# A hybrid GLA/S5/mLSTM layer: head pieces resumed by stated waiting times instead of fixed program points

## The chip, the cores and the metric

The kernel runs on one core of one Trainium2 chip. The metric is the device time of one execution in microseconds (us). A profiled execution is also there; its span is the time from its first to its last instruction.

## The reference, cut to what matters

One layer on 1024 tokens of width 1024, all in fp32. The mixer projects the normed input to many parts, runs three branches over them, and adds the branches up with sigmoid gates; a convolutional FFN follows.

```python
z = u @ w_in
(g_q, g_k, g_v, g_lr, g_r, s_u, m_q, m_k, m_v, m_i, m_f, m_o, gate_pre) = jnp.split(z, ...)
o = gla_chunked(heads(g_q), heads(g_k), heads(g_v), heads(log_a))      # 4 heads, chunks of 64
o = rms_norm(o, gla_norm) * silu(heads(g_r))
y = gelu(s5_scan(s_u, ...))                 # 32 groups: complex diagonal recurrence, 64 states each
y = y * sigmoid(y @ s5_w_glu + s5_b_glu)
qk = silu(causal_dwconv(concatenate([m_q, m_k]), ml_conv_w, ml_conv_b))
hid = mlstm_chunked(q_ml, k_ml, heads(m_v), m_i + ml_b_i, m_f + ml_b_f)    # 4 heads
hid = sigmoid(heads(m_o)) * hid
merged = gates[0] * (o @ gla_w_proj) + gates[1] * (y @ s5_w_proj) + gates[2] * (hid @ ml_w_proj)
x = x + rms_norm(merged @ w_out);  x = x + rms_norm(conv_ffn(rms_norm(x)))
```

## The kernel before, in words

Every projection is done in three fp32r matmuls, from a rounded part ("hi") and a rest ("lo") of each operand. ACT casts hi and DVE subtracts to get lo; `split` (lines 87 to 89) does both, and `load_w` (line 91) loads a weight tile by DMA and splits it whole. The raw tile has one buffer, hi and lo have two each.

The stretch that the change touches goes from about 76 to 616 us. TensorE has there a *main stream* of projections, in this order: the S5 input (`su_half` twice, token-major, line 864); for each of four GLA heads K, Q and the output gate R (`chan_major`, line 117: 8 blocks of 6 matmuls of 512 columns, 48 in all, into one PSUM pair of two banks); the mLSTM values (two halves of 8 token tiles, `tok_mm`, line 179); for each of four mLSTM heads K, Q and the output gate O; then the merge gates, in pairs of 128 columns, first by plain products (96 matmuls a pair), later in a seven-product form (84 matmuls a pair, `run`). PSUM has eight banks: two pairs (`big`), three single banks (`bank`) and one for S5 (`bank2`).

Beside it run *pieces*: Python generators that are stepped at fixed places of the main stream and trace a few instructions each time, until their next `yield`.
- `gla_gates(h)` (line 329), not a generator: two matmuls into a PSUM pair, then DVE and ACT work on 1024 columns that gives the decay factors E. It is traced whole, at one place.
- `gla_inner` (line 359): transposes of k (line 368), scores (374), chunk states (384, with fifteen DVE state updates in line 394), inner outputs (400), outer outputs (410), a sum on DVE (412), a square on POOL (413), the norm (415 to 417), and last the output transposes (423). It is stepped four times with TensorE work.
- `ml_gates` (line 444): a chain of tiny matmuls and DVE instructions (498 and 495 among them) that gives the mLSTM weights.
- `conv_silu2` (line 522): the convolution, one ACT instruction, three on DVE that read the PSUM pair (line 527), a tanh and a last one on DVE; traced whole behind each K and Q of the mLSTM.
- `ml_inner` (line 543): transposes (552), scores (559), states (568, 571), outputs (579, 580, with 582 and 584 on DVE) and output transposes (597). Stepped four times.
- `s5_set(s)` (line 702), eight sets of four groups: seven small loads; products on POOL (723 to 737); two small scalings on DVE (732, 733); transposes (742, 746); the kernel block (752, 753); the rotation angles, with rounding on DVE (767, 768) and the sums on POOL (`sub` and `add`, lines 610 and 607), two sines on ACT (773, 774), a square on POOL and a scaling on DVE (776); the input product (781); the *rotation* on DVE: nine products and sums (line 789) and eight scans (799); the products 812 and 816; and after each second set two output transposes (825) with a gelu.

What sets the order: `advance()` steps every running generator once, after each projection and after each fourth token tile; `extra()` steps S5 alone, at every projection's middle, as often as a rate of 0.6 allows:

```python
def extra():
    credit[0] += RATE
    if credit[0] >= 1.0 and s5 in running:
        credit[0] -= 1.0
        step([s5])
```

The compiler's scheduling pass then places each engine's instructions: by program order, but an instruction whose inputs are late by the pass's own times can be overtaken by later ones. The gates' loop goes on by plain products while any generator runs (`while running`, line 1051).

Of the kernel before, what the change touches and what calls it, by code (L numbers as in the profile page):

```python
# [18 lines left out]
S = 1024  # L19
# [3 lines left out]
H = 4  # L23
# [9 lines left out]
def hybrid_layer(ctx: ExitStack, tc: tile.TileContext, a, out, dbg=None):  # L33
# [53 lines left out]
    def split(hi, lo, src):  # L87
        return (ordered("act", act.copy(hi, src)),  # L88
                ordered("dve", dve.tensor_tensor(lo, src, hi.bitcast(F32), op=ALU.subtract)))  # L89

    def load_w(srcs, rows, cols, late=None, keep=None):
# [5 lines left out]
        if late is None:  # L97
            split(hi, lo, raw)
        else:
            late.append((hi, lo, raw))  # L100
# [16 lines left out]
    def chan_major(wt, i, xh, xl, ps=None, ns=(0, 1)):  # L117
# [14 lines left out]
    midway = []  # L132
# [7 lines left out]
    RATE = 0.6  # L140
# [38 lines left out]
    def tok_mm(wt, i, lhs, put, c0, to=None):  # L179
        hi, lo = wt  # L180
        ps = big()[:, 0, 0:hi.shape[2]] if to is None else to([128, hi.shape[2]])
        for k in range(8):
            for p, (l, r) in enumerate(((0, hi), (1, hi), (0, lo))):
                pe.matmul(ps, lhs(l, k, i), r[:, k, :],
                          start=(k == 0 and p == 0), stop=(k == 7 and p == 2))
        put(i, c0, ps)

# [141 lines left out]
    def gla_gates(h):  # L329
        ps = big()  # L330
        for n in range(2):
            pe.matmul(ps[:, n, :], wg[:, h * 128:(h + 1) * 128], lrx[:, n * 512:(n + 1) * 512],
                      start=True, stop=True)
        z = flat(ps)
        bias = cols[:, 40 + h:41 + h]
        ax, mn, b = g([128, S]), g([128, S]), g([128, S])
        dve.tensor_scalar(mn, z, bias, 0.0, op0=ALU.add, op1=ALU.min)
        dve.scalar_tensor_tensor(out=ax, in0=mn, scalar=2.0, in1=z, op0=ALU.mult, op1=ALU.subtract)
# [12 lines left out]
        return ax, b, mn, dec  # L351

    def silu2(ps):
# [3 lines left out]
        return t  # L357

    def gla_inner(h, E, r2):
        qd, ki, kd, dec = E  # L360
        vt = g([128, 8, 128])
        sync.dma_start(vt, v_dram[0][:, :, h * 128:(h + 1) * 128].rearrange("i p e -> p i e"))
        kt = g([128, 8, 128])
        for hf in range(2):
# [4 lines left out]
            act.copy(kt[:, hf * 4:hf * 4 + 4, :], ps)  # L369
        for hf in range(2):  # L370
# [5 lines left out]
        yield  # L376
        st = [g([128, 8, 128]) for _ in range(2)]
        pool.memset(st[0][:, 0, :], 0.0)
        for o in range(2):
            for p in range(2):  # L380
# [7 lines left out]
                else:  # L388
                    act.copy(st[o][:, 2::2, :], kv[:, 0:3, :])
                    if o == 0:  # L390
                        act.copy(st[1][:, 0, :], kv[:, 3, :])
            for c in range(o * 8, min(o * 8 + 8, 15)):
# [9 lines left out]
        yield  # L402
        yield
        for hf in range(2):
# [8 lines left out]
            pool.tensor_tensor(sq, oo, oo, op=ALU.mult)  # L413
            ssq = small.tile([128, 4], F32, tag="ssq4", name="ssq4")
            dve.tensor_reduce(ssq, sq, axis=AX.X, op=ALU.add)
            rs = rstd_of(ssq, 4, DH)
            dve.tensor_tensor(oo, oo, rs.unsqueeze(2).to_broadcast([128, 4, 128]), op=ALU.mult)
        yield
        yield
# [24 lines left out]
    def ml_gates():  # L444
# [18 lines left out]
        act.activation(e1, e1, AF.Ln, bias=1.0)  # L463
        dve.tensor_scalar(lf, xf, 0.0, None, op0=ALU.min)
        dve.tensor_tensor(lf, lf, e1, op=ALU.subtract)
        yield
# [9 lines left out]
        yield  # L476
# [6 lines left out]
        yield  # L483
# [12 lines left out]
        yield  # L496
# [10 lines left out]
        yield  # L507
# [14 lines left out]
    def conv_silu2(ps, j):  # L522
        z = flat(ps)
        acc, t = g([128, S]), g([128, S])
        act.activation(acc, z, AF.Identity, scale=cols[:, 24 + j:25 + j], bias=cols[:, 32 + j:33 + j])
        for k in range(1, 4):
# [3 lines left out]
        act.activation(t, acc, AF.Tanh, scale=0.5)  # L530
        dve.scalar_tensor_tensor(out=t, in0=t, scalar=1.0, in1=acc, op0=ALU.add, op1=ALU.mult)
        return t
# [10 lines left out]
    def ml_inner(h, wm, qm, km, tm):  # L543
# [4 lines left out]
        for e in range(2):  # L548
            ps = bank([128, 4, 128])
            for q in range(4):  # L550
# [3 lines left out]
                              kwx[:, h, e * 4:e * 4 + 4].unsqueeze(2).to_broadcast([128, 4, 128]), op=ALU.mult)  # L554
        for e in range(2):
# [6 lines left out]
        yield  # L562
        st = g([128, 8, 129])
        pool.memset(st[:, 0, :], 0.0)
        for j0, n in ((0, 3), (3, 3), (6, 1)):
# [3 lines left out]
            act.copy(st[:, j0 + 1:j0 + 1 + n, :], kv[:, 0:n, :])  # L569
            for j in range(j0, j0 + n):  # L570
                dve.scalar_tensor_tensor(out=st[:, j + 1, :], in0=st[:, j, :], scalar=scx[:, h, j:j + 1],
                                         in1=st[:, j + 1, :], op0=ALU.mult, op1=ALU.add)
        yield
        nn = g([128, 8, 129])
        for j0, n in ((0, 3), (3, 3), (6, 2)):
# [8 lines left out]
            dve.tensor_tensor(dst, dst, pa[:, 0:n, :], op=ALU.add)  # L584
        rd = small.tile([128, 8], F32, tag="rd", name="rd")
# [7 lines left out]
        yield  # L593
        for e in range(2):
# [4 lines left out]
            dve.scalar_tensor_tensor(out=tm[0][:, t], in0=tm[0][:, t], scalar=1.0,  # L599
                                     in1=po.rearrange("p a b -> p (a b)"), op0=ALU.add, op1=ALU.mult)  # L600
        sync.dma_start(o_dram[2][h], tm[0])
# [99 lines left out]

    def s5_set(s):
# [11 lines left out]
        bst = s5p.tile([128, 2, 4, 16], F32, tag="bst", name="bst", bufs=1)  # L714
        for i, nm, p0 in ((0, "s5_b_re", 0), (0, "s5_b_im", 64), (1, "s5_b_im", 0), (1, "s5_b_re", 64)):
            sync.dma_start(bst[p0:p0 + 64, i], a[nm][0, gs].rearrange("g p h -> p g h"))
        cl = s5p.tile([64, 3, 64], F32, tag="cl", name="cl", bufs=1)
        for i, nm in ((0, "s5_c_re"), (1, "s5_c_im"), (2, "s5_c_re")):
            sync.dma_start(cl[:, i, :], a[nm][0, gs].rearrange("g h p -> (g h) p"))
# [7 lines left out]
        pool.tensor_copy(zr_, zt.rearrange("p j (g h) -> p g j h", h=16)[:, :, ::-1, :])  # L727
        ps = bank2([128, 2, 64])
# [3 lines left out]
        dve.tensor_scalar(c01[:, 0].rearrange("p g h -> p (g h)"), ps[:, 0, :], sgn[:, 0:1], None, op0=ALU.mult)  # L732
# [844 lines left out]
```

## Time and profile before

| | us |
|---|---|
| median of 3 runs (lowest, highest) | 1746.9 (1745.06, 1747.82) |
| the profiled execution's own time | 1745.36 |
| its span | 1743.6 |
| TensorE, DVE, ACT, POOL busy | 1689.5, 1151.8, 646.8, 398.1 |
| mean granted TensorE clock | 0.994 of 2.4 GHz |

Engines are named PE (TensorE), PEld (TensorE's weight load), DVE (VectorE), ACT (ScalarE), POOL (GpSimd) and SPq (SyncE's DMA queue). A line such as L816 is a line of the kernel. A fp32 tile is named by its pool's tag: z is a PSUM pair, m a single bank, q a buffer of S5 (in PSUM or SBUF), g one of the 14 head buffers. A row of the waits reads: this engine and line waited for that engine and line; total, times, longest. A row of busy times gives, behind the stretch and its length, busy us (and instructions) of PE, PEld, DVE, ACT and POOL, then the mean granted clock, the DMA share and GB/s. In a row of groups, "busy, mean ns of one" is followed by the idle time just before and what ended it.

### The profile page before, as it was taken

How to read it: one execution, taken by the hardware profiler on the slowest of the kernel's cores; microseconds unless marked ns; L12 is line 12 of the kernel's file. 1: busy time of each engine (PE TensorE's matmuls, PEld its weight loads, DVE VectorE, ACT ScalarE, POOL GpSimd, SP SyncE). 2: the span in 40 equal slices, each digit the busy share in tenths (PEclk: the TensorE clock that was granted, in tenths of full speed). 3: DMA queues.
4: the chain of work that ended last, by engine and by line, in shares of the span. 5: the costliest groups of instructions: out<-in, count | busy, mean ns of one | idle time of the engine just before them, and what ended most of it. 6: DMA issues, size and time to landing. Idle time of an engine off the chain costs nothing. (4 is left out here: it accounts for less than half of the span.)

```text
span 1743.6 us, 21877 instructions
## 1 busy us (share of the span) xinstructions
PE 1689.5 (97%) x8556; PEld 1412.1 (81%) x8556; DVE 1151.8 (66%) x1462; ACT 646.8 (37%) x940; POOL 398.1 (23%) x437
## 2 busy tenths in 40 slices
PE   6999998999999999999899999999999999999997
PEld 6997877897888888888688788788888888888886
DVE  4426677536667675444745654967777787669987
ACT  4544533333443223333510233433333333344343
POOL 1163243333334012222000011022322332101021
PEclk9999999999999999999899999999999999999999
DMA  6242131333141322434674643222232223483161
GB/s 205 68 113 60 43 88 34 92 91 89 23 133 49 97 85 85 127 115 145 222 249 144 217 142 125 73 73 82 76 90 79 85 73 97 169 283 127 55 218 54
DMA packets 196440, 195.10 MB, mean 112 GB/s; under 512 B 29208, under 2 KB 154305, under 8 KB 196337
## 3 DMA queue, kind: packets, MB, share of 16 engines
q1 hardware_dynamic: 195456, 190.56, 34.9%
q0 software_dynamic: 880, 3.15, 0.5%
q8 instruction: 67, 1.10, 0.3%
q14 instruction: 37, 0.30, 0.1%
HBM read 143.32 MB, written 48.25 MB: 110 GB/s over the span
## 5 line engine op out<-in xcount | busy, mean ns | idle before, releaser
L89 DVE TENSOR_TENSOR lo<-raw,hi 128x512 fp32r<-128x512 f32 (+3 forms) x163 | 174.7, 1091 | 132.0 <-ACT hi L88 129.3
L88 ACT CAST hi<-raw 128x512 fp32r<-128x512 f32 (+3 forms) x163 | 130.2, 833 | 283.1 <-PE z L126 122.0
L983 POOL TENSOR_TENSOR raw<-raw 128x512 f32<-128x512 f32 x28 | 39.5, 1412 | 472.4 <-DVE lo L89 472.4
L126 PE MATMUL z<-ohl,hi 128*128 128x512 f32 x448 | 123.3, 398 | 6.1 <-ACT ohl L1098 6.1
L126 PEld LDWEIGHTS z<-ohl,hi 128*128 128x128 f32 x448 | 85.5, 191 | 26.1 <-ACT ohl L1098 6.5
L68 POOL TENSOR_SCALAR rstd<-ssq 128x1 f32<-128x1 f32 (+1 forms) x32 | 9.3, 292 | 316.4 <-ACT x L1262 262.5
L126 PE MATMUL z<-u0h,hi 128*128 128x512 f32 x240 | 79.5, 408 | 1.4 <-DVE g L894 1.4
L126 PE MATMUL z<-u0h,lo 128*128 128x512 f32 x240 | 77.0, 398 | 0.0
L126 PE MATMUL z<-u0l,hi 128*128 128x512 f32 x240 | 76.5, 398 | 0.0
L126 PE MATMUL z<-u1h,hi 128*128 128x512 f32 x240 | 75.4, 395 | 0.0
L126 PE MATMUL z<-u1h,lo 128*128 128x512 f32 x240 | 75.0, 392 | 0.0
L126 PE MATMUL z<-u1l,hi 128*128 128x512 f32 x240 | 74.9, 393 | 0.0
L126 PE MATMUL z<-ohl,lo 128*128 128x512 f32 x224 | 70.2, 396 | 0.0
L1303 DVE SCALAR_TENSOR_TENSOR cv<-u,fcol,cv 128x1023 f32<-128x1023 f32 (+1 forms) x38 | 48.7, 1280 | 23.9 <-ACT cv L1301 23.9
L89 DVE TENSOR_TENSOR xl<-raw,xh 128x512 fp32r<-128x512 f32 x57 | 51.8, 935 | 11.2 <-ACT xh L88 8.3
L1301 ACT ACTIVATE cv<-u,fcol 128x1024 f32<-128x1024 f32 x19 | 23.6, 1244 | 89.9 <-DVE u L1001 89.9
L789 DVE TENSOR_TENSOR q<-q,q 128x512 f32<-128x512 f32 x72 | 49.5, 714 | 8.7 <-PE q L812 8.3
L126 PEld LDWEIGHTS z<-u0h,lo 128*128 128x128 f32 x240 | 45.3, 190 | 9.7 <-issue 0.2
L126 PEld LDWEIGHTS z<-u1h,lo 128*128 128x128 f32 x240 | 45.1, 188 | 9.8
L126 PEld LDWEIGHTS z<-u1l,hi 128*128 128x128 f32 x240 | 44.9, 188 | 9.9 <-issue 0.2
L126 PEld LDWEIGHTS z<-u0l,hi 128*128 128x128 f32 x240 | 44.8, 189 | 9.6 <-issue 0.4
L126 PEld LDWEIGHTS z<-u1h,hi 128*128 128x128 f32 x240 | 44.5, 188 | 9.3
(561 smaller groups left out, 5006.0 us busy)
## 6 DMA issues: line engine op xcount, KB each, us to landing
raw<-in_w_in_dram SPq DMA_DIRECT2D x48, 512.0 KB, 5.3
pt<-gate SPq DMA_DIRECT2D x24, 512.0 KB, 3.3
raw<-in_ffn_w_up_dram SPq DMA_DIRECT2D x22, 512.0 KB, 4.0
raw<-in_ffn_w_gate_dram SPq DMA_DIRECT2D x22, 512.0 KB, 5.3
h<-cv SPq DMA_DIRECT2D x21, 512.0 KB, 2.6
bx<-in_ffn_w_down_dram SPq DMA_DIRECT2D x15, 512.0 KB, 4.4
by<-in_ffn_w_down_dram SPq DMA_DIRECT2D x15, 512.0 KB, 5.1
gate<-u SPq DMA_DIRECT2D x11, 512.0 KB, 3.0
```

What stands on the lines that cost most here:

```text
L68: pool.tensor_scalar(r, ssq, 1.0 / width, EPS, op0=ALU.mult, op1=ALU.add)
L88: return (ordered("act", act.copy(hi, src)), ordered("dve", dve.tensor_tensor(lo, src, hi.bitcast(F32), op=ALU.subtract)))
L89: ordered("dve", dve.tensor_tensor(lo, src, hi.bitcast(F32), op=ALU.subtract)))
L126: pe.matmul(ps[:, n, :], l[:, k, c], r(k, n), start=(k == 0 and p == 0), stop=(k == nk - 1 and p == 2))
L789: dve.tensor_tensor(o, x, y, op=op)
L983: pool.tensor_tensor(a22, a21, a22, op=ALU.add)
L1301: first = act.activation(cv, src, AF.Identity, scale=fcol[:, 44 + f:45 + f], bias=fcol[:, 66 + f:67 + f])
L1303: ins = dve.scalar_tensor_tensor(out=cv[:, k:], in0=src[:, 0:S - k], scalar=fcol[:, (2 - k) * 22 + f:(2 - k) * 22 + f + 1], in1=cv[:, k:], ...
```

## The change

Each `yield` of a piece now returns the waiting time in us before its next part. A modelled clock `now` is moved on by the main stream (`tick`: 1.37 us per block of six matmuls, 1.45 us per half token tile) and by 0.13 us for each TensorE instruction of a piece. At each tick up to two pieces that are due are resumed. The first TensorE and the first DVE instruction that a resumed piece traces are ordered behind the newest instruction of that engine; the weight splits are left out of this. So pieces can't be placed ahead of where they were traced.

```diff
+            for k in range(0, rows, rows // 2):            # load_w: split by halves
+                ks = slice(k, k + rows // 2)
+                split(hi[:, ks, :], lo[:, ks, :], raw[:, ks, :])
...
-            if k == 3 and midway:                          # chan_major, after each block k
-                midway[0]()
+            tick(6 * len(ns) * 0.114)
...
+    def note(first=None):
+        traced = nc.cur_bb.bb.instructions
+        bound, work = set(), 0.0
+        for ins in traced[seen[0]:]:
+            e = ins.engine
+            if e == mybir.EngineType.PE:
+                work += 0.13
+            if e not in (mybir.EngineType.PE, mybir.EngineType.DVE):
+                continue
+            if first is not None and e not in bound and e in newest:
+                bound.add(e)
+                tc.add_manual_dep(ins, newest[e], ..., reason="turn")
+            if ins.name not in free_:
+                newest[e] = ins.name
+        seen[0] = len(traced)
+        return work
+
+    def resume(turn_):
+        note()
+        try:
+            wait = next(turn_[1])
+        except StopIteration:
+            turns.remove(turn_)
+            wait = 0.0
+        now[0] += note(turn_)
+        turn_[0] = now[0] + wait
+
+    def tick(us):
+        now[0] += us
+        due = sorted((t for t in turns if t[0] <= now[0]), key=lambda t: t[0])
+        for t in due[:2]:
+            resume(t)
```

`gla_gates` becomes a generator. Its projection goes through two single banks of 512 columns instead of a pair; after the first exp and ln it waits 8.0. `gla_inner` is cut into more parts: k transposes, 4.0, scores, 1.5, states of the first half, 2.5, their updates and the second half's states, 2.5, updates and inner outputs, 10.0, outer outputs, 3.5, sums of squares, 7.0, norm, 5.0, output transposes. The square is made by ACT instead of POOL. `ml_gates` waits 6.0 once and 5.0 between its steps. `silu2` waits 2.5 between its tanh and its DVE instruction.

```diff
+    def conv_silu2(ps, j, to):
...
         act.activation(acc, z, AF.Identity, scale=cols[:, 24 + j:25 + j], bias=cols[:, 32 + j:33 + j])
+        yield 2.5
         for k in range(1, 4):
             dve.scalar_tensor_tensor(out=acc[:, k:], in0=z[:, 0:S - k], ...
         act.activation(t, acc, AF.Tanh, scale=0.5)
+        yield 8.0
         dve.scalar_tensor_tensor(out=t, in0=t, scalar=1.0, in1=acc, op0=ALU.add, op1=ALU.mult)
+        yield 3.0
+        to.append(t)
```

`ml_inner` begins with the convolution of K; then come the transposes, 1.5, the scores (when q is there), 1.5, states, 3.0, state updates, 5.0, the outputs of three, three and two chunks with 1.5 between, 7.0, and the output transposes, when the output gate is there. In `s5_set` the angles move to the front, the rotation's preparation goes to DVE and ACT, and the parts get times:

```diff
+        mul(ph, iob.to_broadcast(sq_), t_hi[:, gs].unsqueeze(2).to_broadcast(sq_))
+        mul(pl, iob.to_broadcast(sq_), t_lo[:, gs].unsqueeze(2).to_broadcast(sq_))
...
+        yield 4.0
+        for i in range(2):
+            dve.tensor_scalar(pk, ph, magic, None, op0=ALU.add)
+            dve.tensor_scalar(pk, pk, -magic, None, op0=ALU.add)
+            dve.tensor_tensor(ph, ph, pk, op=ALU.subtract)
+            if i == 0:
+                dve.tensor_tensor(ph, ph, pl, op=ALU.add)
...
+        act.activation(cs, cs, AF.Square)
+        act.activation(cs, cs, AF.Identity, scale=-2.0, bias=1.0)
...
-        dve.tensor_scalar(c01[:, 0].rearrange("p g h -> p (g h)"), ps[:, 0, :], sgn[:, 0:1], None, op0=ALU.mult)
+        act.mul(c01[:, 0].rearrange("p g h -> p (g h)"), ps[:, 0, :], sgn[:, 0:1])
...
+        yield 8.0
...
-            sub(ph, ph, pk)
-            if i == 0:
-                add(ph, ph, pl)
-        mul(cs, cs, cs)
-        dve.tensor_scalar(cs, cs, -2.0, 1.0, op0=ALU.mult, op1=ALU.add)
```

Behind the transposes (one of them now in a single bank) it waits 3.0, behind the kernel block 6.0; then come the products 812 and 781 (781 in a single bank), 4.0, the rotation and the loads of the next set, 15.0, and the product 816, 2.5. The output transposes become a piece of their own, with 3.0 between the two. S5 is started ahead of `su_half(0)`, with 20.0 after its tables. In the main stream:

```diff
         pk = flat(chan_major(wt, 0, u_hi, u_lo))
-        advance()
+        finish_turn(gates.pop(0))
...
-        E = gla_gates(h + 1) if h + 1 < H else None
+            gates.append(spawn(gla_gates(h + 1, E), 6.0))
...
-            tok_mm(wt, i, tok_lhs, put_dram(v_dram[1]), hf * 256, None)
+            tok_mm(wt, i, tok_lhs, put_dram(v_dram[1]), hf * 256, bank if hf == i == 0 else None)
...
+        spawn(ml_inner(h, wm, ps, of, made_tm[h]))
         ps = chan_major(wt, 1, u_hi, u_lo)
+        spawn(conv_silu2(ps, h, of))
+        if h in (0, 3):
+            ow = col_tiles(w_in, [C_MO + h // 2 * 256, C_MO + h // 2 * 256 + 128])
...
+        for j in ((0,), (1,), (), (2, 3))[h]:
+            ml_out(ow, j)
...
-    while running:
+    while turns:
```

`ml_out(ow, j)` is the projection of head j's output gate and its tanh. `advance`, `extra`, `pump` and `RATE` are gone.

## Rows read from the trace of the kernel before

**Rows 1.** page, busy time of each engine; granted TensorE clock in 40 slices.

```profile
PE 1689.5 (97%) x8556; PEld 1412.1 (81%) x8556; DVE 1151.8 (66%) x1462; ACT 646.8 (37%) x940; POOL 398.1 (23%) x437
...
PEclk9999999999999999999899999999999999999999
```

**Rows 2.** busy time by stretch: start:end and length, then each engine, PEclk.

```profile
76.00:616.60 540.60, 519.24 (x3250) 447.12 (x3249) 337.03 (x525) 217.70 (x314) 186.14 (x218) 0.99 0.28 76
123.50:328.00 204.50, 192.02 (x1109) 157.18 (x1108) 139.13 (x206) 84.92 (x112) 79.53 (x80) 0.98 0.23 61
239.50:292.00 52.50, 49.59 (x299) 41.69 (x298) 33.88 (x48) 22.72 (x30) 14.25 (x18) 0.97 0.20 53
292.00:328.00 36.00, 31.98 (x183) 25.37 (x183) 24.39 (x38) 10.79 (x13) 16.39 (x18) 0.95 0.27 77
```

**Rows 3.** waits of TensorE, 76 to 616.6 us: us in total, times, longest.

```profile
PE q L816 <- DVE q L789: 7.4, 5, 3.2
PE m L368 <- DVE g L412: 3.5, 2, 2.8
PE m L580 <- DVE g L582: 1.9, 3, 0.7
PE z L184 <- DVE g L356: 1.6, 1, 1.6
PE q L816 <- POOL rstd L68: 1.5, 1, 1.5
PE z L126 <- DVE g L894: 1.4, 1, 1.4
PE m L498 <- DVE g L495: 1.1, 1, 1.1
```

**Rows 4.** timeline, DVE and TensorE, around the two longest waits.

```profile
295.98 1.58 DVE L789 TENSOR_TENSOR q<-q,q 128x512 f32<-128x512 f32 x1
...
297.70 1.38 PE L816 MATMUL q<-q,q 128*128 128x128 f32 x8 [3.20 <-DVE q L789]
...
271.72 1.11 PE L368 MATMUL m<-ident,g 128*128 128x128 f32 x4 [2.80 <-DVE g L412]
```

**Rows 5.** groups by line and form, 76 to 616.6 us, DVE and POOL.

```profile
L789 DVE TENSOR_TENSOR q<-q,q 128x512 f32<-128x512 f32 x72 | 49.5, 714 | 8.7 <-PE q L812 8.3
...
L799 DVE TENSOR_TENSOR_SCAN q<-r,q 128x128 f32<-128x128 f32 x64 | 21.8, 412 | 0.0
L767 DVE TENSOR_SCALAR q<-q 128x512 f32<-128x512 f32 x16 | 13.2, 826 | 39.5 <-POOL q L604 23.1 <-POOL q L607 11.4 <-POOL q L786 5.1
...
L527 DVE SCALAR_TENSOR_TENSOR g<-z,cols,g 128x1023 f32<-128x1023 f32 x8 | 10.2, 1276 | 0.6 <-ACT g L525 0.6
...
L610 POOL TENSOR_TENSOR q<-q,q 128x512 f32<-128x512 f32 x16 | 20.6, 1290 | 18.9 <-DVE q L768 18.9
...
L607 POOL TENSOR_TENSOR q<-q,q 128x512 f32<-128x512 f32 x8 | 11.2, 1402 | 0.6
```

**Rows 6.** undisturbed stretch (columns of rows 2); timeline behind an S5 piece.

```profile
650.00:700.00 50.00, 50.00 (x220) 41.04 (x220) 26.30 (x39) 18.68 (x29) 13.39 (x11) 1.00 0.28 85
...
260.61 0.71 PE L126 MATMUL z<-u1h,hi 128*128 128x512 f32 x2
...
261.62 0.63 PE L126 MATMUL z<-u1h,lo 128*128 128x512 f32 x2
```

**Rows 7.** groups of the weight splits on DVE, 76 to 616.6 us.

```profile
L89 DVE TENSOR_TENSOR lo<-raw,hi 128x2048 fp32r<-128x2048 f32 x15 | 35.4, 2357 | 10.6 <-ACT hi L88 10.6
...
L89 DVE TENSOR_TENSOR lo<-raw,hi 128x1024 fp32r<-128x1024 f32 x6 | 7.3, 1220 | 10.0 <-ACT hi L88 10.0
```

**Rows 8.** DMA issues: KB each, us to landing.

```profile
gate<-g SPq DMA_DIRECT2D x2, 512.0 KB, 6.0
```

**Rows 9.** timeline, ACT, around a table load.

```profile
265.12 1.28 ACT L773 ACT_TABLE_LOAD   x1
266.42 0.72 ACT L773 ACTIVATE q<-q,sgnpi 128x512 f32<-128x512 f32 x1
```

More of the change, by code (lines that the diff above doesn't have):

```diff
@@ L87, in split @@
     def split(hi, lo, src):
-        return (ordered("act", act.copy(hi, src)),
+        made = (ordered("act", act.copy(hi, src)),
                 ordered("dve", dve.tensor_tensor(lo, src, hi.bitcast(F32), op=ALU.subtract)))
+        free_.update(i.ins.name for i in made)
+        return made
     def load_w(srcs, rows, cols, late=None, keep=None):
@@ L185, in tok_mm @@
                           start=(k == 0 and p == 0), stop=(k == 7 and p == 2))
+            if k == 3:
+                tick(1.45)
         put(i, c0, ps)
+        tick(1.45)
     def tok_lhs(l, k, i):
@@ L327, in hybrid_layer, with gla_gates @@
     dve.tensor_copy(wg[64:96, :], wgl[64:96, :].bitcast(F32))
[L329 to L334, printed above, removed]
+    def gla_gates(h, E):
         bias = cols[:, 40 + h:41 + h]
         ax, mn, b = g([128, S]), g([128, S]), g([128, S])
-        dve.tensor_scalar(mn, z, bias, 0.0, op0=ALU.add, op1=ALU.min)
-        dve.scalar_tensor_tensor(out=ax, in0=mn, scalar=2.0, in1=z, op0=ALU.mult, op1=ALU.subtract)
+        for n in range(2):
+            t = slice(n * 512, (n + 1) * 512)
+            z = bank([128, 512])
+            pe.matmul(z, wg[:, h * 128:(h + 1) * 128], lrx[:, t], start=True, stop=True)
+            dve.tensor_scalar(mn[:, t], z, bias, 0.0, op0=ALU.add, op1=ALU.min)
+            dve.scalar_tensor_tensor(out=ax[:, t], in0=mn[:, t], scalar=2.0, in1=z, op0=ALU.mult, op1=ALU.subtract)
         act.activation(ax, ax, AF.Exp, bias=ngk[:, h:h + 1])
         act.activation(ax, ax, AF.Ln, bias=1.0)
+        yield 8.0
         dve.tensor_tensor(mn, mn, ax, op=ALU.subtract)
@@ L401, in gla_inner @@
             act.copy(os_[hf][:, 0], pa)
-        yield
-        yield
+        yield 10.0
+        sums = []
         for hf in range(2):
@@ L541, in ml_weights, with ml_inner @@
         return wm
-    def ml_inner(h, wm, qm, km, tm):
+    def ml_inner(h, wm, ps, of, tms):
+        made = []
+        yield from conv_silu2(ps, 4 + h, made)
+        km = made[0]
         vx = g([128, 8, 129])
@@ L569, in ml_inner @@
             act.copy(st[:, j0 + 1:j0 + 1 + n, :], kv[:, 0:n, :])
+        yield 3.0
+        for j0, n in ((0, 3), (3, 3), (6, 1)):
             for j in range(j0, j0 + n):
@@ L592, in ml_inner @@
         dve.tensor_tensor(hd, nn[:, :, 0:128], rd.unsqueeze(2).to_broadcast([128, 8, 128]), op=ALU.mult)
-        yield
+        yield 7.0
+        while not tms:
+            yield 1.0
+        tm = tms[0]
         for e in range(2):
@@ L700, in s5_base, with s5_load @@
         pool.tensor_scalar(g_i, g_i, sgn[:, 0:1], -1.0, op0=ALU.mult, op1=ALU.mult)
+    s5_in = []
+    def s5_load(s):
+        gs = slice(s * 4, s * 4 + 4)
+        bst = s5p.tile([128, 2, 4, 16], F32, tag="bst", name="bst", bufs=1)
+        for i, nm, p0 in ((0, "s5_b_re", 0), (0, "s5_b_im", 64), (1, "s5_b_im", 0), (1, "s5_b_re", 64)):
+            sync.dma_start(bst[p0:p0 + 64, i], a[nm][0, gs].rearrange("g p h -> p g h"))
+        cl = s5p.tile([64, 3, 64], F32, tag="cl", name="cl", bufs=1)
+        for i, nm in ((0, "s5_c_re"), (1, "s5_c_im"), (2, "s5_c_re")):
+            sync.dma_start(cl[:, i, :], a[nm][0, gs].rearrange("g h p -> (g h) p"))
+        return bst, cl
     def s5_set(s):
@@ L743, in s5_set @@
         act.copy(bv, ps)
-        ps = bank2(sq_)
+        ps = bank(sq_)
         for q in range(4):
@@ L803, in s5_set @@
         vtt(xx[:, :, 1:129], w1, t1, ALU.subtract)
-        yield
-        yield
-        if s % 2 == 0:
-            ysp.append(s5p.tile([128, 8, 128], F32, tag="ys", name="ys", bufs=1))
-        ys = ysp[-1]
-        dst = ys[:, :, c0:c0 + 64].rearrange("p j (g h) -> p g j h", h=16)
-        ps = bank2(sq_)
-        for q in range(4):
-            pe.matmul(ps[:, q, :], ut[:, q, :], tt[:, q, :], start=True, stop=True)
-        act.copy(dst, ps.rearrange("p q (j h) -> p q j h", h=16))
+        if s < 7:
+            s5_in.append(s5_load(s + 1))
+        yield 15.0
         ps = bank2(sq_)
@@ L867, in su_half @@
             tok_mm(wt, i, tok_lhs, put_dram(su_dram), hf * 256, bank)
-            if i % 4 == 3:
-                advance()
-            if i == 1 and mid:
-                mid()
+            if i == 1 and hf == 0:
+                gates.append(spawn(gla_gates(0, E)))
+                spawn(ml_gates(), 10.0)
         su_done.append(hf)
```

187 lines of the change are left out of this document (89 added, 98 removed).

## The prediction

> **What bounds the kernel now.** I read the page's busy shares first. TensorE is busy for 1689.5 of 1743.6 us, DVE for 1151.8, and TensorE's granted clock is full in nearly every slice [rows 1]. So whatever is to be won is time in which TensorE stands still, or runs at the lower clock. Next I cut the stretch that the change touches (from the first S5 projection, at 76 us, to the last head piece, at 616.6 us) by stage. There TensorE stands still for 540.6 - 519.2 = 21.4 us [rows 2]. More than half of it, 204.5 - 192.0 = 12.5 us, lies in the GLA stage (123.5 to 328 us). In that stage the granted clock is also 0.97 for 52.5 us and 0.95 for 36 us, that is about half of full speed (1.2 instead of 2.4 GHz) for some 3.4 us in each, or 52.5 x 0.03 + 36 x 0.05 = 3.4 us of lost work [rows 2].
>
> Third, the waits of TensorE in that stretch, by line. Seven groups make 7.4 + 3.5 + 1.9 + 1.6 + 1.5 + 1.4 + 1.1 = 18.4 of the 21.4 us, and the last engine to arrive is nearly always DVE [rows 3]. The worst is line 816, the S5 output matmul, which waits for the rotation: 7.4 us, and 1.5 us more that the view puts down to POOL, 8.9 in all. The timeline shows how it comes about. DVE does nine products and sums and eight scans; its last product stands at 295.98 us, and the matmul that reads it starts at 297.70 us after 3.20 us of waiting [rows 4]. DVE was not short of time before: over the stage it is busy 139 of 204.5 us [rows 2]. The pieces of the heads and of S5 come at fixed program points, sometimes too close behind each other. The low clock follows such a wait each time: the other long one is line 368, 2.80 us at 271.72 [rows 4].
>
> So the ceiling is 21.4 + 3.4 = 24.8 us, 1.4% of the time. Nothing after 616 us changes but the weight splits.
>
> **The change, part by part**, against the profiled execution's own 1745.4 us (span 1743.6). It is 1.5 us under the median of the runs.
>
> *Waiting times instead of program points.* TensorE does the same matmuls and transposes; only their places change.
> - Line 816: the rotation costs DVE 9 x 0.714 + 8 x 0.412 = 9.7 us [rows 5], and the new code leaves 15 us of modelled TensorE time between the rotation and the matmul. That leaves 5.3 us for other DVE work that gets in front. I take it that a quarter of the 8.9 us stays: 2.2. Bounds: 0 and all of it.
> - Line 368: the transposes of one head wait for a PSUM bank that the DVE sum of line 412 of another head must give back. The pieces now stand apart, but the gate projections and two S5 results join the same three banks. Half stays: 1.7 of 3.5. Bounds 0 and 3.5.
> - Line 580 (the mLSTM outputs, whose three steps are now 1.5 us apart): a third stays, 0.6 of 1.9.
> - Line 184 behind line 356 (1.6), line 126 behind line 894 (1.4) and line 498 (1.1): these go. The first token tile of the mLSTM values takes a bank instead of the PSUM pair that the GLA gate still holds; the GLA gate projection no longer takes a pair; the scalar chain of the mLSTM gates gets 5 us between its steps.
> - Of the rest, 21.4 - 18.4 = 3.0 us in short pieces, half stays: 1.5.
> That is 6.0 us left of 21.4. What is late next I can't see in this trace; new waits on the three banks and behind DVE bursts I put at 4 us, between 0 and the 12.5 us of the GLA stage today (more than that is the first rival). So 10.0 instead of 21.4: **-11.4 us**.
>
> *The clock.* Both low stretches follow waits of 2.8 us and more. If no wait is that long they go: **-3.4 us**. Bounds 0 and -3.4.
>
> *More pieces.* A GLA head's TensorE work comes in 7 pieces instead of 4, an mLSTM head's in 7 instead of 4, and an S5 set's in one more, with the two output transposes of each pair of sets apart: 12 + 12 + 8 + 4 = 36 more returns to the main stream. Where the stream runs undisturbed it makes 220 matmuls in 50 us, 0.227 us each; four matmuls right behind an S5 piece take 261.62 - 260.61 = 1.01 us instead of 0.91 [rows 6]. So 0.1 us a return: **+3.6 us**. Bounds 0 (a piece that meets another costs none) and twice that.
>
> *Rotation on DVE.* Three sums of 8 sets leave POOL (20.6 + 11.2 us) and cost DVE 24 x 0.714 = 17.1 us [rows 5]; DVE loses the scaling of line 776 and the two of lines 732 and 733, and POOL two squares, to ACT. DVE's total rises by at most 17 us over a stretch of 500 us. The cover is DVE's idle time, 65 us in the GLA stage alone; so I cost it at nothing by itself. POOL gets earlier with it: the waits of line 767 for POOL (39.5 us of DVE idle time) shrink. ACT takes the squares and scalings in its own idle time; its instructions in front of a wanted copy are a rival below.
>
> *Weights split by halves.* Two pieces cost DVE 2 x 1.220 instead of 2.357 us, and ACT two casts instead of one [rows 7]. The 23 loads touched lie beside matmuls of other weights, and no wait of TensorE on a weight is among the rows: nothing. Without that cover it would be 0.08 us each. The later half of a load can be handed over later without TensorE noticing.
>
> *S5 loads earlier, sets started with the first projection.* The seven small loads of a set are issued in front of the wait instead of behind it. On SP they stand in front of the output and weight loads that follow; each waits for buffers whose readers are long through. Nothing.
>
> *Output gates last.* Heads 2 and 3 of the mLSTM run their output projections (2 x 48 x 0.227 = 22 us) behind the last q, so the last head's chain has matmuls beside it. Adding up its stated waits (2.5 + 8 + 3 for the convolution, then 1.5, 3, 5, 1.5, 1.5, 7, each rounded up to a tick of 1.4 us), it ends within the first pair of standard gate products; before, one pair is needed too (two gate tiles leave from the heads' buffers [rows 8]). Nothing; if a second pair were needed, 96 matmuls would replace 84 of the seven-product form: 12 x 0.227 = +2.7 us.
>
> Sum: 1745.4 - 11.4 - 3.4 + 3.6 = 1734.2 us, and with the 1.5 us by which the profiled execution is under the median, **1736 us**.
>
> **Rivals.**
> *The PSUM pairs come back late.* TensorE's main stream has two pairs, so a projection of 48 x 0.227 = 10.9 us can start only when DVE has read out the one before last. The new code puts the convolution's DVE part (3 x 1.276 = 3.8 us, [rows 5]) behind a tick and a stated 2.5 us, 4.1 us after the projection's end instead of right behind it; what is queued in front of it then holds the pair. If that is a whole rotation, the pair is back after 4.1 + 9.7 + 3.8 = 17.6 us: 6.7 us of TensorE waiting. The gate of the GLA output is put off in the same way, with one instruction of some 1.3 us: 4.1 + 9.7 + 1.3 - 10.9 = 4.2 us. With about four rotations beside GLA heads and three beside mLSTM heads that is up to 4 x 4.2 + 3 x 6.7 = 36.9 us, and 7 x 1.7 = 11.9 us of low clock behind them. At half the rotations it is 24 us: 1736 + 24 = 1760 us. It decides at a quarter of them, where 12 us take back what is won. For it: every long wait of today is on DVE, and sets that start closer together put more bursts beside the heads. Against: the rotation's seventeen instructions are handed over one by one, DVE is idle for a third of the stage [rows 2], and today no wait on a pair behind the convolution is among the rows.
> *The waits only change places.* The ordering holds an instruction back, it doesn't make DVE faster, and the compile-time pass still places instructions by its own times, so that the stated waits may not be what stands on the chip. Then the clock alone gains: about 1745 us as a median.
> *ACT reloads its tables.* A switch between functions costs ACT 1.28 us, and the sine of line 773 starts right behind it, 0.02 us later [rows 9]. Finer pieces alternate more often. One more switch in front of a copy that TensorE waits for, in each of 8 sets and 4 heads, is 12 x 1.28 = 15.4 us: 1736 + 15 = 1751 us. Against it: none of the long waits of today ends with ACT [rows 3]. The Trainium skill (ScalarE: Activation LUTs, Table sets: the hidden batching unit) speaks against a change like this one: it wants calls batched by table set, and puts a switch at about 2.7 us with its drain, by which the estimate would be 32 us. The row has the sine start where the load ends, so the measured 1.28 us decides.
>
> **How the numbers follow.** Forecast 0.66, late pairs 0.17, waits moved 0.11, tables 0.06. A measurement of this kernel can tell 0.2% (3.5 us) from no change. Faster takes the forecast, 0.66; the moved waits are within that bound, 0.11, and half of the tables, 0.03, so the same has 0.14; slower has 0.17 + 0.03 = 0.20. The lower end is the ceiling: 1745.4 - 24.8 + 1.5 = 1722 us. The upper end takes in the moved waits and the tables: 1751 us. That leaves out the late pairs and the little that may lie under the ceiling.
>
> **What would show it.** Idle TensorE time from 76 us to the end of the head pieces near 10 instead of 21.4 us; line 816 under 3 us; a granted clock of 1.00 through the GLA stage; DVE above its 68% there; the eighth S5 set done well before the last mLSTM head's chain; still two gate tiles from the heads' buffers. It is wrong if line 816, the banks or the pairs still hold TensorE for more than 15 us, or if ACT's table loads are what the copies in front of TensorE wait for.

## The result and the profile after

The kernel after takes **1734.97 us** as a median of 5 runs (1729.41 to 1736.92), beside 1747.82 us of the kernel before on the same chip: ratio **0.9927**, 95% interval 0.9914 to 0.9941, so 0.6 to 0.9% faster. Measured once more beside the experiments (the control, below) it took 1737.86 us, ratio 0.9939 (0.9926 to 0.9952); both figures belong to it. The forecast was 1736 us.

First the page of the kernel after: busy time of each engine, and the granted clock in 40 slices.

```profile
span 1733.0 us, 21935 instructions
PE 1689.0 (97%) x8556; PEld 1413.1 (82%) x8556; DVE 1179.9 (68%) x1493; ACT 664.4 (38%) x1002; POOL 351.8 (20%) x397
...
PEclk9999999999999999999999999999999999999999
```

TensorE's work is the same to half a microsecond (1689.5 before, [rows 1]); its idle time over the span falls from 1743.6 - 1689.5 = 54.1 to 1733.0 - 1689.0 = 44.0 us. As the matmuls are the same, a difference of two spans is always such a sum: idle time, here -10.1 us, and busy time, which is longer where the same matmuls run at the lower clock, here -0.5 us. The experiments are read in the same way. DVE carries 28 us more, POOL 46 us less. Next the stretches, in the columns of [rows 2]: the whole head stretch, which now ends at 601.2 us, and the GLA stage.

```profile
78.00:601.20 523.20, 510.12 (x3215) 440.49 (x3213) 361.14 (x546) 230.81 (x363) 140.63 (x179) 1.00 0.28 77
131.00:331.00 200.00, 193.75 (x1146) 160.61 (x1145) 150.44 (x224) 89.17 (x135) 59.17 (x62) 0.99 0.23 61
```

TensorE is idle for 523.2 - 510.1 = 13.1 us instead of 21.4, and DVE is busy for 75% of the GLA stage instead of 68%. The waits of TensorE in the head stretch (us in total, times, longest):

```profile
PE m L425 <- DVE g L385: 2.6, 2, 1.7
PE m L481 <- DVE g L474: 2.5, 1, 2.5
PE m L617 <- DVE g L592: 2.3, 1, 2.3
PE m L229 <- ACT ev L243: 1.8, 2, 1.3
PE m L628 <- DVE g L592: 1.3, 2, 0.8
...
PE m L651 <- DVE g L653: 0.6, 1, 0.6
```

Line 903, the old line 816 with 8.9 us of waiting [rows 3], is not in the list at all. What is there now are single waits at places that hardly waited before: the scores (425) for a bank that the gate projection's sums on DVE hold, the GLA output transposes (481) behind the normalization, the k transposes (617) and scores (628) of an mLSTM head behind the end of its convolution.

By landmarks (first instruction of each stage, both profiled executions): from the first S5 projection to the first product of the seven-product form it is 655.49 - 76.50 = 579.0 us before and 648.03 - 78.15 = 569.9 us after, **9.1 us won in the heads**. In the control it was 648.84 - 79.03 = 569.8. A further 3.1 us were won in front of the first products of the last mixing stage, and 1.65 us lost in the start-up: -9.1 - 3.1 + 1.65 = -10.6 us, the difference of the spans. TensorE's wait at that second place, in the kernel before, in after and in the control:

```profile
PE z L126 <- ACT ohl L1098: 6.1, 1, 6.1
PE z L130 <- ACT ohl L1157: 3.0, 1, 3.0
PE z L130 <- ACT ohl L1157: 5.2, 1, 5.2
```

The last two are the same kernel, so this gain isn't the change's alone.

### The profile page after: what moved, and what is told of

It reads as the page before. It is cut to its first block, busy times and chain, and to the rows that moved or that the text cites. A ratio compares the mean times of both kernels' runs of the same rounds, so it can differ in the third digit from the quotient of the medians.

```text
span 1733.0 us, 21935 instructions
## 1 busy us (share of the span) xinstructions
PE 1689.0 (97%) x8556; PEld 1413.1 (82%) x8556; DVE 1179.9 (68%) x1493; ACT 664.4 (38%) x1002; POOL 351.8 (20%) x397
## 5 line engine op out<-in xcount | busy, mean ns | idle before, releaser
L89 DVE TENSOR_TENSOR lo<-raw,hi 128x512 fp32r<-128x512 f32 (+2 forms) x186 | 183.2, 1006 | 126.4 <-ACT hi L88 123.6
L88 ACT CAST hi<-raw 128x512 fp32r<-128x512 f32 (+2 forms) x186 | 133.6, 753 | 284.6 <-PE z L130 135.3
L1044 POOL TENSOR_TENSOR raw<-raw 128x512 f32<-128x512 f32 x28 | 39.5, 1410 | 490.4 <-DVE lo L89 396.1
L1494 PE MATMUL z<-lo,hi 128*128 128x512 f32 x132 | 51.3, 393 | 0.4 <-DVE lo L89 0.4
```

The costliest lines, as they stand in the source:

```text
L88: made = (ordered("act", act.copy(hi, src)), ordered("dve", dve.tensor_tensor(lo, src, hi.bitcast(F32), op=ALU.subtract)))
L1044: pool.tensor_tensor(a22, a21, a22, op=ALU.add)
L1494: pe.matmul(ps, l[:, e, c], r[:, 2 + e, :], start=(first and e + i == 0), stop=(last and e == n - 1 and i == 2))
```

## The experiments

Twelve runs; line numbers are those of the kernel after unless it says otherwise, ratios are to the kernel before. They ran in three lots, each beside the kernel before, which took 1747.7, 1747.0 and 1747.4 us. The control, the kernel after unchanged, belongs to the first lot.

> The kernel after, unchanged, so that its ratio to the kernel before is taken on the same chip as the other three: 0.993 (1735 us against 1748), between 0.991 and 0.994; TensorE idle for 13 us between 78 and 601 us, line 903 without a wait.

Measured: 1737.86 us (1735.88 to 1738.77), ratio 0.9939. The waits in the head stretch are those shown above to a tenth (line 651 has 1.1 us in two waits). The head gain repeats; start-up and the last stage's boundary differ by some 3 us between two executions of one kernel. Times below are set against this 1738. The two medians of this one kernel, 1735.0 and 1737.9 us, lie 2.9 us apart, so a smaller difference tells nothing by itself.

**The stated time ahead of line 903.**

```diff
-        yield 15.0
+        yield 3.0
         ps = bank2(sq_)
```

> One stated time alone: 3 us instead of 15 between the rotation on DVE and the S5 output matmul of line 903. Theory (the stated waiting time is what removed the old wait of line 816): the rotation takes 9.7 us of DVE, so the matmul comes 6 us too early in each of eight sets, less what it would have waited in the queue; some 4 to 6 us of wait in most sets, 20 to 40 us of TensorE idle time at line 903 and low clock behind the long ones: 1755 to 1780 us, slower than the kernel before. Rival 1 (the compile-time order, not the stated time, sets where the matmul stands): within 3 us of 1735. Rival 2 (partly covered, as in the kernel before): waits of about 9 us at line 903 and 1 to 3 us of low clock, about 1746 us.

Measured: **1765.75 us**, ratio 1.0098 (1.0082 to 1.0114). Waits of TensorE in the head stretch:

```profile
PE q L903 <- DVE q L883: 12.7, 8, 2.6
PE z L229 <- ACT ev L243: 5.0, 1, 5.0
PE z L130 <- DVE g L405: 4.2, 1, 4.2
PE z L130 <- DVE g L587: 3.2, 1, 3.2
```

All eight sets wait at line 903, so the stated time is what removed the old wait, and the first rival falls. The time lies in the theory's range, but not for the theory's reason: line 903 waits 12.7 us and not 20 to 40, nearer to the second rival's 9. The rest of the price of 28 us stands elsewhere. Three waits for PSUM pairs, none of them in the control, make 12.4 us more, and the mean granted clock of the run is 0.987 instead of the control's 0.994. TensorE is idle for 1764.2 - 1699.1 = 65.1 us instead of 1736.7 - 1690.0 = 46.7, and busy 9.1 us longer: 18.4 + 9.1 = 27.5 us, the difference of the spans.

**The rotation's sums and cosine on POOL again.**

```diff
-            dve.tensor_tensor(ph, ph, pk, op=ALU.subtract)
+            sub(ph, ph, pk)
...
-                dve.tensor_tensor(ph, ph, pl, op=ALU.add)
+                add(ph, ph, pl)
...
-        act.activation(cs, cs, AF.Square)
-        act.activation(cs, cs, AF.Identity, scale=-2.0, bias=1.0)
+        mul(cs, cs, cs)
+        dve.tensor_scalar(cs, cs, -2.0, 1.0, op0=ALU.mult, op1=ALU.add)
```

> The three sums of a set's rotation angles go back to POOL, and the square and the scaling of the cosine to POOL and DVE, as in the kernel before. Theory (the prediction costed this part at nothing): 1735 us within 2 us, POOL busy some 40 us more, DVE some 10 us less, and TensorE's idle time in the head stretch within 2 us of 13. Rival (POOL's chain was a cause of the late rotation; its results arrive late again, and TensorE waits at line 903): 3 to 9 us slower, with waits at line 903 whose last arrival is POOL or ACT's sine.

Measured: **1763.23 us**, ratio 1.0081 (1.0064 to 1.0098): 25 us slower, where the theory had nothing. The rival had the size too small and the place wrong: line 903 has no wait. TensorE waits longer at other lines (in the control the first has 2.6 us, the second 1.3, the third none):

```profile
PE m L425 <- DVE g L385: 5.3, 2, 2.8
PE m L628 <- DVE g L592: 4.3, 3, 2.5
PE q L851 <- ACT q L841: 3.4, 2, 3.1
```

New among DVE's waits are those for POOL, and the timeline shows one case of how they reach TensorE (start, us, then in brackets what it waited for):

```profile
DVE q L825 <- POOL q L680: 32.1, 7, 7.9
DVE q L816 <- POOL q L683: 27.9, 8, 6.5
```

```profile
482.75 1.21 DVE L89 TENSOR_TENSOR lo<-raw,hi 128x1024 fp32r<-128x1024 f32 x1
...
486.48 1.04 POOL L680 TENSOR_TENSOR q<-q 128x512 f32<-128x512 f32 x1 [1.35 <-ACT q L823]
...
487.55 0.43 DVE L825 TENSOR_SCALAR q<-q 128x512 f32<-128x512 f32 x1 [3.59 <-POOL g L610]
...
490.92 1.22 DVE L592 SCALAR_TENSOR_TENSOR g<-g 128x1024 f32<-128x1024 f32 x1
...
492.19 1.48 PE L617 MATMUL m<-ident,g 128*128 128x128 f32 x8 [3.70 <-DVE g L592]
```

The scaling of line 825 waits for POOL's square (line 680, ending at 487.52; the view names the POOL instruction behind it), and that for ACT's sine of line 823. It stands at the head of DVE's queue, DVE is idle for 3.59 us, and eight instructions of other pieces come late, the convolution's end of line 592 among them, for which TensorE then waits 3.70 us (2.3 in after and its control). The Trainium skill (Perfetto Trace Analysis: Tensor Engine Instruction) says that DVE's queue is strictly first in, first out; the trace agrees with the row above. In the whole head stretch DVE stands 60.0 us waiting for POOL at these two lines, and the 3.6 of this case besides. Against the control TensorE is idle for 1760.9 - 1702.1 - 46.7 = 12.1 us more and busy for 1702.1 - 1690.0 = 12.1 us more, at a mean clock of 0.986: in this execution the lower clock costs as much again as the waits, where in the run with the short stated time it was half as much (9.1 to 18.4). ACT may have a share that no run separates: its copy of line 841, which line 851 waits for, stands behind the sines.

**The two parts of that, one at a time.** Only the sums on POOL:

> Half of the second run above: the three sums of the rotation angle alone go back to POOL, while the cosine's square and scaling stay on ACT. In the run with both parts DVE stood 60 us waiting for POOL at the sums and their neighbours, with everything behind it in its queue. Theory (DVE's queue is held by POOL's turn in the middle of the chain): nearly all of those 25 us come back, 1755 to 1763 us, with DVE waiting more than 40 us for POOL at the two lines of the sums. Rival (the square on POOL and the scaling on DVE behind it hold the queue): within 4 us of the control's 1738.

Measured: 1743.12 us (1736.70 to 1746.31), ratio 0.9974 (0.9960 to 0.9989): 5 us. DVE's wait at the sums is the same 27.9 us, so that theory is wrong by four fifths, and the wait by itself isn't what costs. Only the square and the scaling:

> The other half of the second run: only the cosine's square goes back to POOL and its scaling to DVE; the three sums stay on DVE. With both parts the time was 25 us above the control, with the sums alone 5. Theory (the scaling is queued on DVE right behind the sums, and waits there for ACT's sine and then POOL's square with the whole queue behind it): the rest of the 25 us, 1753 to 1760 us, with 25 us and more of DVE waiting for POOL at the scaling. Rival (the two waits only hurt where they stand behind each other in one set): within 5 us of the control's 1738.

Measured: 1745.73 us (1738.53 to 1752.21), ratio 0.9987 (0.9968 to 1.0005): 8 us.

```profile
DVE q L825 <- POOL q L680: 31.0, 8, 8.2
```

Again the full wait on DVE, at a third of the price; the executions of this run spread over 14 us, and its interval is 3 us to either side. Alone the two parts cost 5 and 8 us, together 25: neither expectation holds. What fits is that a piece's stated time has some slack, which one wait of 3 to 4 us uses up and two in one set exceed; that step is argued, and no run shows it by itself.

**The sums alone, in the kernel before** (its lines 769 and 771, to DVE):

> One part of the change alone in the kernel before: the three sums of the rotation angle on DVE instead of POOL, nothing else. There DVE stands 46.8 us waiting for POOL in the head stretch, 34.5 us of them at line 767. Theory (that wait is a cause of the late DVE results which TensorE waits for, with the old program points too): idle time of TensorE falls from 21.4 to 10 to 16 us, 1738 to 1744 us. Rival 1 (DVE's wait for POOL only hurts where pieces stand at the new times): 1747 within 2 us. Rival 2 (the earlier rotation collides with other DVE work): 1750 us or more.

Measured: 1744.00 us, ratio 0.9985 (0.9974 to 0.9997): 3 us of the 11. TensorE's waits there, and the longest of DVE's for POOL:

```profile
PE q L816 <- DVE q L789: 7.4, 5, 3.2
PE m L374 <- DVE g L412: 1.9, 1, 1.9
...
PE q L816 <- POOL rstd L68: 1.5, 1, 1.5
...
PE m L368 <- DVE g L412: 1.0, 1, 1.0
...
DVE q L767 <- POOL q L604: 23.1, 6, 11.3
```

Line 816 keeps its 8.9 us to the tenth, so that wait isn't one of POOL's sums; the stated 15 us removed it, as the first experiment shows. Line 368 falls from 3.5 to 1.0 us, but line 374 now waits 1.9 us for the same sum of line 412. TensorE is idle for 17.8 us of the head stretch instead of 21.4, outside the theory's 10 to 16; its time is met at the weak end. And the edit took away less than the theory thought: of the 39.5 us in which DVE stood at line 767, the 23.1 us behind POOL's products (line 604, `mul`) are still there [rows 5]. What those cost in the kernel before, no run shows.

**The order edges left out** (the call to add_manual_dep in note).

> The order edges between a resumed piece and the instructions recorded before it on TensorE and DVE are left out; stated times and pieces stay. Theory (the stated times do the work, the edges only hold the instructions where they were written): the compile-time pass hoists some of them, the time is within 4 us of 1735, and the start-up gains back 1.5 us because the transposes of the S5 base can run ahead of the projection again. Rival (the edges are what keeps the stated times on the chip): the waits of the kernel before come back, TensorE idle above 20 us in the head stretch, 1743 to 1750 us.

Measured: 1741.58 us, ratio 0.9961 (0.9946 to 0.9976), 3.7 us behind the control and 6.6 above the 1735 of the theory, between it and the rival. The waits are fewer and longer:

```profile
PE m L476 <- DVE g L380: 4.8, 1, 4.8
PE m L646 <- DVE g L648: 4.2, 1, 4.2
PE m L447 <- ACT g L433: 3.6, 1, 3.6
```

(Lines are five lower here.) With the shorter ones they make 16.9 us, between after's 12.9 and the rival's 20. So the stated times alone keep two thirds of the control's gain, 6 of 10 us. The start-up didn't gain back: its first projection stands at 79.3 us, so the order isn't what moved it.

**Weights split whole again.**

```diff
-            for k in range(0, rows, rows // 2):
-                ks = slice(k, k + rows // 2)
-                split(hi[:, ks, :], lo[:, ks, :], raw[:, ks, :])
+            split(hi, lo, raw)
```

> The kernel after with each weight split in one piece again. The profile of after showed 3.1 us less waiting in front of the first products of the last mixing stage, and the control 1 us less. Theory (the halves gain nothing that a measurement can tell; that boundary varies from one execution to the next): within 2 us of the control's 1738. Rival (the halves let DVE start its subtraction earlier and gain at that boundary): 1740 to 1742 us, with 6 us of waits there instead of 3 to 5.5.

Measured: **1731.07 us** (1724.60 to 1735.76), ratio 0.9909 (0.9888 to 0.9931), the fastest kernel of this study. Its waits in the head stretch (lines two lower) and at the boundary:

```profile
PE m L423 <- DVE g L383: 2.7, 2, 1.8
...
PE m L479 <- DVE g L472: 1.4, 1, 1.4
PE m L626 <- DVE g L590: 1.3, 2, 0.8
PE m L615 <- DVE g L590: 1.2, 1, 1.2
...
PE z L128 <- DVE ohl L1158: 0.5, 1, 0.5
```

The rival, as it was put, falls: the boundary has 0.5 us with whole splits. But the boundary doesn't follow the splits at all: it has 6.1 us in the last run below, with whole splits too, and 0.5 us in the next two runs, with halves. So the 4.7 us by which it is shorter here than in the control can't be credited to the splits. The heads take 644.16 - 79.49 = 564.7 us against 569.9, with no stretch of the heads at the lower clock; the profile is of an execution of 1727.3 us, 3.8 under the median. The interval still touches the control's, so that this part of the change costs anything is likely from this run and not yet shown.

**Output projections in the old order** (one behind each head's q).

> The kernel after with the four output projections of the mLSTM in the old order, one behind each head's q. Theory (the prediction costed this part at nothing): within 2 us of the control's 1738, still one pair of standard gate products. Rival (without the two projections behind the last q the last head's chain needs a second standard pair, 2.7 us, and its pieces come with nothing else to run beside them): 1741 to 1746 us.

Measured: 1737.05 us, ratio 0.9940 (0.9921 to 0.9958): no difference in the time. Yet the mechanism of the rival is there. The issues of standard gate tiles from the heads' buffers (after, they are two):

```profile
gate<-g SPq DMA_DIRECT2D x4, 512.0 KB, 2.6
```

Four tiles, so a second pair of standard products runs (8568 matmuls instead of 8556). Its 2.7 us don't show in the time. In the same execution TensorE waits 0.5 us at the last stage's boundary where the control waits 5.2, which is more than enough to hide them; whether the second pair brings that about is open. The next run has both too.

**The convolution later.** Line 585, `yield 2.5` to `yield 8.0`.

> One stated time doubled and more: 8 us instead of 2.5 between the end of an mLSTM projection and the convolution on DVE that reads it out of its PSUM pair. Theory (the prediction's first rival has its price right, only its condition did not arise): the pair is back some 8 + 1.4 + 3.8 = 13 us after the projection, 2.3 us later than the 10.9 us of the next one, and what DVE has in front adds to it: 1 to 4 us of waiting in front of most of the eight projections at line 130, 1743 to 1755 us. Rival (the projections have slack, as tanh and the pieces between them push the next one back): within 3 us of 1738, no wait at line 130 above 1 us.

Measured: 1750.19 us (1742.63 to 1753.73), ratio 1.0009 (0.9991 to 1.0026): at the median all the gain is gone.

```profile
PE z L130 <- DVE g L587: 7.6, 3, 2.7
...
PE m L651 <- DVE g L653: 2.1, 1, 2.1
...
PE m L617 <- DVE g L675: 2.0, 1, 2.0
```

The pairs come back late in three of eight projections, the longest by 2.7 us where the working gave 2.3; a second standard pair was needed too. So the first rival of the prediction counted the length of such a wait rightly; its dear case, a whole rotation in front of the convolution, isn't among these rows. The profile is of an execution of 1744.1 us: four of the ten took 1742.6 to 1744.1, six 1749.8 to 1753.7, and what those six lose beyond it no profile shows.

**An attempt at something faster**: three stated times longer where after still waits.

```diff
-        yield 5.0
+        yield 7.0
         while r2[0] is None:
...
-        yield 3.0
+        yield 5.0
         to.append(t)
...
-            gates.append(spawn(gla_gates(h + 1, E), 6.0))
+            gates.append(spawn(gla_gates(h + 1, E), 9.5))
```

> Three stated times moved by 2 to 3.5 us where after still waits: the GLA gate projection from 6 to 9.5 us behind the head's start, the step in front of the GLA output transposes from 5 to 7, the end of the convolution from 3 to 5. Theory (a wait goes where its stated time grows past DVE's lateness, and each costs its own length): the waits of lines 425, 481 and 617 (2.6, 2.5 and 2.3 us) shrink to 2 us in all, 1732 to 1735 us. Rival (waits only change places: the pieces collide elsewhere): within 2 us of 1738, with as much idle time at other lines.

Measured: 1745.22 us, ratio 0.9990 (0.9979 to 1.0000), 7 us slower. In the GLA stage it does what it should: the waits of 425 and 481 are gone, and TensorE is idle there (78 to 331 us) for 253.0 - 248.65 = 4.35 us instead of 253.0 - 244.52 = 8.5:

```profile
78.00:331.00 253.00, 248.65 (x1590) 212.88 (x1589) 176.00 (x274) 124.57 (x192) 80.51 (x113) 0.99 0.26 71
```

Behind it more is lost. Waits of TensorE from there on, and the timeline at the second one:

```profile
PE m L651 <- DVE g L653: 4.4, 2, 2.9
PE z L229 <- DVE g L405: 2.6, 1, 2.6
PE q L869 <- DMA q<-kt: 2.4, 1, 2.4
PE m L617 <- DVE g L592: 2.3, 1, 2.3
```

```profile
337.25 5.51 DVE L446 SCALAR_TENSOR_TENSOR g<-g,dec 128x128 f32<-128x128 f32 x7
342.68 1.21 DVE L405 SCALAR_TENSOR_TENSOR g<-g,z 128x1024 f32<-128x1024 f32 x1
...
343.95 0.58 PE L229 MATMUL z<-hi,u0h 128*128 128x256 f32 x1 [2.63 <-DVE g L405]
```

Seven state updates of the last GLA head stand on DVE in front of line 405, the last step of the output gate's silu, which reads a PSUM pair that TensorE's line 229 then waits for. The wait of 617 that the third time was to end is as long as ever. The same with whole splits:

> The same three times, and each weight split in one piece, as in the third run of the second lot, which came out at 1731 us and left the boundary in front of the last mixing stage with 0.5 us of waiting. Theory (the halves cost some 4 us, in ACT's and DVE's queues): 4 us below the run with the times alone, 1727 to 1731 us, the fastest of all. Rival (the 1731 was the spread between executions): as fast as the run with the times alone, within 2 us.

Measured: 1744.52 us, ratio 0.9983 (0.9974 to 0.9992). It isn't the fastest; 0.7 us below the run with halves, within the rival's 2 us. Its wait at the last stage's boundary, with whole splits:

```profile
PE z L128 <- ACT ohl L1155: 6.1, 1, 6.1
```

With whole splits the three times cost 13 us, with halves 7. So the halves are priced at 0.7 us by one pair of runs and at 7 by the other, and in the profiles of the latter, 11.1 us apart, 4.7 us are the boundary; their size stays open. The first and third time together with whole splits, without the convolution's, wasn't tried.

## Why the prediction was right, point by point

**The bound** held: the same work on TensorE, and what was won are idle time and clock. The heads gave 9.1 of a ceiling of 24.8 us.

**Waits**: -11.4 us predicted, 21.4 - 13.1 = -8.3 measured. The old waits went further than I had them: line 816 from 8.9 to nothing (2.2 predicted), line 368 from 3.5 to nothing under its new number (1.7), line 580 from 1.9 to 1.0 (0.6). (In brackets is what was to be left.) The term that was too small is the new waits, put at 4 us: lines 425, 481, 617, 628 and 452 make 2.6 + 3.2 + 2.3 + 1.3 + 0.5 = 9.9 us. Their kind was named: the gate projections joined the three banks, and 425 waits for just that.

**Clock**: -3.4 predicted, -1.7 measured. No wait in the heads reaches 2.8 us any more, so the condition was met, and one low stretch is left all the same: 10 x (1 - 0.83) = 1.7 us, at the 2.5 us wait of line 481. The clock of the GLA stage is 0.99 and not the 1.00 that was to show it.

**Returns**: +3.6 predicted; what is left for them is -9.1 + 8.3 + 1.7 = +0.9 us. The lower bound was nearer. This is a remainder, which no run measures by itself: an estimate from one disturbed return was taken for all.

**Rotation on DVE at nothing**: this is the step that failed in its reason. The sum added at most 17 us of DVE work (361.1 us in the heads against 337.0 are 24), found it covered by idle time, and saw POOL's part only as a wait of 39.5 us that would "shrink". Undone, it costs 25 us, and leaves a kernel with all the stated times that is slower than the kernel before (1.0081); its sums alone win 3 us in the kernel before. DVE's idle time was no free cover: 39.5 us of it were spent standing at line 767, and an instruction that stands there holds what is queued behind it, as the timeline of that run shows. Only the part of those 39.5 us behind the sums was removed by moving them; the products now come earlier, with 4 us stated behind them, and no run prices that. The Trainium skill (Trainium Architecture — The Big Picture: The five engines, in one table) puts streaming elementwise work on POOL at twice DVE's time; here it is 1290 against 714 ns [rows 5], 1.8 times.

**Weight halves at nothing**: not shown to be wrong. The upper bound, 0.08 us for each of 23 loads, is 1.8 us; the runs without them are 0.7 and 7 us faster, and the second figure is in doubt. **Output gates at nothing**: right as a sum. The reason given was too short: with the stated times and the old order a second pair runs, as the side case had it, so the move does save one, though its 2.7 us don't show in the time. **S5 loads and start**: the eighth set's output stands at 574.9 us instead of 584.0, 26 us before the heads' end instead of 33: well before the last chain, as it was to show, but no earlier against it than in the kernel before.

**What I didn't have**: the boundary of the last mixing stage (-3.1 us) and the start-up (+1.65). Together they are -1.5 us, and the control shows that both vary between executions.

**The rivals.** Late pairs didn't arise: no wait at line 130 in the heads. The run with the late convolution shows that 5.5 us more of stated time brings them. That the waits only change places held in part: 9.9 us of new ones for 18.4 of old; in the run with three moved times two waits end and others cost more. Table loads did not multiply: ACT makes 33 in the heads instead of 34, and only 2.3 us of after's waits end with ACT. The forecast was right within 2 us by both measurements, and part of that is luck: terms too large on one side (waits, clock) and on the other (returns) met an unforeseen 1.5 us.

## What to carry to other kernels

Price an engine that waits by what stands in its queue behind the waiting instruction, not by its idle time: DVE's 60 us behind POOL took 25 us from TensorE, half of it as work at the lower clock, and 28 or 31 us of the same waits took 5 or 8. A stated time between producer and consumer removes a wait when it covers the producer's chain: 15 us behind a rotation of 9.7 us of DVE work left no wait, 3 us left 12.7. After that every such time is tuned against the others, and lengthening three of them to end their own waits lost more elsewhere. Before believing a boundary, look at it in a second execution of the same kernel.

## What the runs showed that was not expected

The same wait comes with the low clock in one execution and without it in another. After and its control both hold line 481 for 2.5 us near 270 us; the stretch from 268 to 278 us and a later one, after first and the control second:

```profile
268.00:278.00 10.00, 8.61 (x47) 7.66 (x48) 7.12 (x10) 3.49 (x3) 1.86 (x3) 0.83 0.53 164
465.00:475.00 10.00, 7.71 (x56) 6.05 (x55) 8.94 (x15) 4.61 (x8) 0.10 (x2) 1.00 0.63 157
```

```profile
268.00:278.00 10.00, 7.77 (x50) 6.78 (x50) 8.62 (x12) 3.49 (x3) 2.70 (x3) 1.00 0.55 164
465.00:475.00 10.00, 7.70 (x44) 6.51 (x43) 7.90 (x14) 4.45 (x7) 0.00 (x0) 0.83 0.59 152
```

The clock is 0.83 in the one (a third of the stretch at 1.2 GHz) and 1.00 in the other; the control has its 0.83 later, at the 2.3 us wait of line 617, where after has 1.00. So which wait comes with a low stretch, each worth 1.7 us, differs between two executions of one kernel. That this is part of the spread of 3 to 14 us that the kernels here show over their runs is likely and not shown.

The other surprise was that two queue waits on DVE, which alone cost 5 and 8 us, cost 25 us together.
